# Two halves of shift and scale summed as columns instead of as a row, and eleven stores moved to GpSimd's queue

## The chip, the cores and the metric

The kernel runs on one core of a Trainium2 chip. TensorE (PE) multiplies matrices, VectorE (DVE) and ScalarE (ACT) work on the results, GpSimd (POOL) adds weights, and SyncE (SP) starts most transfers. Each engine runs its own instructions in the order in which the program has them, and waits for the others by semaphores. The metric is the device time of one execution in microseconds (us).

## The reference, cut to what matters

One layer of a diffusion backbone over 1024 latent tokens (and 256 context tokens, which go through the same weights) of 1024 channels. Each sub-layer is normed and modulated by a shift, a scale and a gate, nine rows of 1024 that come from a vector `c`:

```python
mod_lat = (jax.nn.silu(c) @ w_mod[layer] + b_mod[layer])[:, None, :]
ml = jnp.split(mod_lat, N_MOD, axis=-1)
...
x = x + 0.5 * ml[2] * swiglu(modulate(rms_norm(x, norm1_g[layer]), ml[0], ml[1]),
                              ffn1_w_in[layer], ffn1_w_out[layer])
...   # attention and short convolution, second SwiGLU
return rms_norm(x, final_g)
```

`modulate(h, shift, scale)` is `h * (1 + scale) + shift`. So the first product of the whole layer needs the shift `ml[0]` and the scale `ml[1]`, each 1024 values made from a 1024 x 1024 block of `w_mod` (4 MB). All of it is float32.

## The kernel before

Channels lie on partitions: `modl[:, m * 8 + k]` is the column of channels `128 k` to `128 k + 127` of row `m`. A half of a row (512 channels, four columns) is made at a time. At the start the order is:

- `first_mod(1, 0)`: the first half of the scale, latent and context at once. PE multiplies eight chunks of 128 input channels into a row of 512 (`ps`), ACT copies the row (`mrow`), and four PE turns (a transpose of one 128-wide piece each) make columns.
- `second_mod(0, 0, raws00, by_pe=4)`: the first half of the shift, latent only. Half of the input chunks (`k` 0 to 3) are summed by DVE: `macc` is `sum over k of silu(c)[k] * rawm[k]`, still spread over 128 partitions. PE does the chunks 4 to 7 as a row. `macc` is split into two parts (`acch` by ACT, `accl`, the remainder, by DVE), PE adds both over the partitions with a column of ones, and ACT's copy and the four turns follow as above. The result goes into `modl` with the bias `bcol`.
- `second_mod(1, 1, raws11)` and `second_mod(0, 1, raws01)`: the second halves, with all eight chunks on DVE (`by_pe=0`), taken in steps between the first products.

Meanwhile `h`, the modulated first tokens (`xtok`, turned by PE into `ps`, `po`, `pt`), becomes `r` (again two parts, `keep`), and the first feed-forward layer starts. It is computed by a scheme with seven half-size products (class `Winograd`) from pairs of weight column blocks. `start_by_half` computes products 1 and 2 of the first 13 pairs ahead of the rest, on chunks of which only half the channels need to be ready: product 1 is copied to `uc[:, 0]`, product 1 + 2 added into `uc[:, 1]` by DVE. Pairs 0 and 1 stay on the chip; the 11 others are stored by `put_aside` to DRAM (`ucd`) and loaded again later. The latter stores go out on SP's queue, the one that also loads the weights `raw`. POOL's first work, apart from the identity, is the sums `s` of weight blocks for the pairs (`pool.tensor_add`).

Most code is written without an order; a scheduler puts each engine's instructions in order from its own estimates, except those that are pinned (`pinned`, `strict`). So an edit can move neighbours. PSUM banks are a further tie: `ps` has five, `pt` two, `po` one, and a bank is given to the next tile only when the last one was read. Every operation is recorded at line 90, that of the helper which issues it; groups are told apart by the tiles' names.

Of the kernel before, what the change touches and what calls it, by code (L numbers as in the profile page):

```python
# [10 lines left out]
F32R = mybir.dt.float32r  # L11
# [7 lines left out]
P = 128  # L19
D = 1024  # L20
KD = D // P
# [30 lines left out]
def tile_dit_layer(  # L52
# [44 lines left out]
    act, dve, pool, pe, sp = (Engine(e) for e in (nc.scalar, nc.vector, nc.gpsimd, nc.tensor, nc.sync))  # L97
# [11 lines left out]
    def uniq(s):  # L109
        n_tiles[0] += 1  # L110
        return f"{s}_{n_tiles[0]}"
# [4 lines left out]
    def ttile(name, n=512, dt=F32):  # L116
        t = tpool.tile([P, 512], dt, tag="t", name=uniq(name))
        return t[:, :n]
# [4 lines left out]
    def ps_s(n=512):  # L123
        return psum.tile([P, 512], F32, tag="s", name=uniq("ps"), bufs=5)[:, :n]

    def ps_t(n=512):
        return psum.tile([P, 512], F32, tag="t", name=uniq("pt"), bufs=2)[:, :n]
# [4 lines left out]
    def matmul(out, w, x, start, stop, pinned=False, on=False):  # L132

        inst = pe.matmul(out, w, x, start=start, stop=stop, skip_group_check=on)
        if pinned:
            tc.keep_in_program_order(inst)

    def transpose(out, in_, pinned=False):
        n = in_.shape[0]
        inst = pe.transpose(out, in_, ident[:n, :n])  # L140
        if pinned:
            tc.keep_in_program_order(inst)
# [9 lines left out]
    ones = const.tile([P, 1], F32, name="ones")  # L152
    dve.memset(ones[:], 1.0)
    ones_r = const.tile([P, 1], F32R, name="ones_r")
# [4 lines left out]
    bcol = const.tile([P, 72], F32, name="bcol")  # L159
# [26 lines left out]
    def col(name, k=0):  # L186
        o = voff[name] + k
        return cols[:, o : o + 1]

    silu_c = const.tile([P, 16], F32, name="silu_c")  # L190
    act.activation(out=silu_c[:], in_=cols[:, :16], func=AF.Silu)

    modl = const.tile([P, 72], F32, name="modl")
# [3 lines left out]
    def split(src, hi, lo, lo_eng=None, hi_eng=None):  # L197

        if hi_eng is dve:
            dve.tensor_copy(out=hi, in_=src)  # L200
        else:
            act.copy(out=hi, in_=src)
        (lo_eng or dve).tensor_sub(out=lo, in0=src, in1=hi.bitcast(F32))
# [21 lines left out]
    def load_cols(w, o, lo_eng=None, pinned=False):  # L225

        return load_w(w[:, o : o + P].rearrange("(k p) n -> p k n", p=P), (KD, P), lo_eng, pinned)
# [97 lines left out]
    def column_adds(m, half, pm, streams):  # L325
        c0 = m * 8 + half * 4
        for i, v in enumerate(streams):
            dve.tensor_add(
                out=(modl, modc)[v][:, c0 : c0 + 4], in0=pm.rearrange("p (k v) -> p v k", v=len(streams))[:, i],
                in1=bcol[:, c0 : c0 + 4],  # L330
            )
# [18 lines left out]
    def second_mod(m, half, raws, by_pe=0):  # L350


        acc, nk = ttile("macc"), KD - by_pe
        for k in range(nk):
            raw, s = raws[k // 2][:, k % 2], silu_c[:, k : k + 1]
            if k:
                dve.scalar_tensor_tensor(out=acc, in0=raw, scalar=s, in1=acc, op0=ALU.mult, op1=ALU.add)
            else:
                dve.tensor_scalar(out=acc, in0=raw, scalar1=s, scalar2=None, op0=ALU.mult)
            yield  # L360
        ah, al = ttile("acch", dt=F32R), ttile("accl", dt=F32R)
        split(acc, ah, al)
        yield
        pr = ps_s()
        for k in range(nk, KD):
            raw, s = raws[k // 2][:, k % 2], silu_c[:, k : k + 1]
            matmul(pr[:1], s, raw, start=k == nk, stop=False, pinned=True)
            if k in (nk, KD - 1):
                yield
        matmul(pr[:1], ones_r[:], ah, start=not by_pe, stop=False)  # L370
        matmul(pr[:1], ones_r[:], al, start=False, stop=True)
        row = ttile("mrow")
        act.copy(out=row[:1], in_=pr[:1])
        yield
        pm = ps_t(4)
        for j in range(4):
            transpose(pm[:, j : j + 1], row[:1, j * P : (j + 1) * P])
        column_adds(m, half, pm, (0,))
        yield

    def norm_gain(name, m, gname):
# [109 lines left out]
    class Winograd:  # L491
# [228 lines left out]

        def put_aside(self, t):
            ucd = dram.tile([P, 2, 512], F32, name=uniq("ucd"))
            sp.dma_start(out=ucd[:], in_=t[:])
            self.started.append(ucd)

        def start_by_half(self):
# [302 lines left out]
    fetched["b"] = fetch_vectors([("b", b_mod[0])])  # L1029
    raws00 = fetch_mod(0, 0)  # L1030
    mod10, mod00 = first_mod(1, 0, raws10), second_mod(0, 0, raws00, 4)

    def column_pairs(w, offsets):
# [41 lines left out]
    for k in range(4):  # L1075
        if k % 2:
            half1.shifted(h0[k][:, 0], k, xh[k])
        else:
            dve.tensor_scalar(
                out=h0[k][:, 0], in0=xh[k], scalar1=gain1["l"][:, k : k + 1], scalar2=modl[:, k : k + 1],  # L1080
# [3 lines left out]
    start = half1.start_by_half()  # L1084
    run(start, 1)
    for k in range(4):
# [3 lines left out]
        else:  # L1090
            dve.tensor_copy(out=h0[k][:, 1], in_=xt)
    mods1 = (step for m, raws in ((1, raws11), (0, raws01)) for step in second_mod(m, 1, raws))
    turn1 = turn_tokens(C1, t1, ("act", "act"))
    for j in range(2, BY_HALF):
# [144 lines left out]
    for d in range(0, KD, 2):  # L1239
        t = ttile("cx")  # L1240
# [3 lines left out]
        for e in range(2):  # L1244
            for token in range(2):
                at = e * CT + token * P
                transpose(pt[:, at : at + P], c_acc[token][:, (d + e) * P : (d + e + 1) * P])
        for e in range(2):
            te = t[:, e * CT : (e + 1) * CT]
            dve.scalar_tensor_tensor(  # L1250
                out=te, in0=pt[:, e * CT : (e + 1) * CT], scalar=gate1["c"][:, d + e : d + e + 1], in1=te, op0=ALU.mult, op1=ALU.add
# [78 lines left out]
    for i in range(KD):  # L1330
# [6 lines left out]
        for ch, bg, gc in mixed():  # L1337
# [4 lines left out]
            for j in (0, 2):  # L1342
# [3 lines left out]
                    out=ya, in0=u[:, a + j - 1 : b + j - 1], scalar=col(f"w{j}", i), in1=ya, op0=ALU.mult, op1=ALU.add  # L1346
# [372 lines left out]
    for ch in (C0, C1):  # L1719
        o = ch[1]  # L1720
        for d in range(KD):
            w = load_cols(w_out[0], d * P)
# [6 lines left out]
                out=xs(d, ch), in0=ps, scalar=modl[:, 40 + d : 41 + d], in1=xs(d, ch), op0=ALU.mult, op1=ALU.add  # L1729
# [12 lines left out]
        out=gf[:], in0=cols[:, voff["gf"] : voff["gf"] + 8], scalar1=math.sqrt(D), scalar2=None, op0=ALU.mult  # L1742
# [132 lines left out]
```

## Time and profile before

| what | value |
|---|---|
| three runs | 2669.2, 2670.65, 2675.72 us (median 2670.65) |
| the profiled execution | 2670.08 us, its span 2668.3 us |
| TensorE busy | 2633.8 us, 13373 matmul records |
| DVE, ACT, POOL busy | 2002.0, 1173.6, 558.4 us |
| mean granted TensorE clock | 0.996 |

The span runs from the first to the last instruction; times in a timeline count from its start. `x8` stands for that many records of one kind in a row, and an f32 matmul that isn't a transpose leaves two records. The bracket at a row's end gives the idle time of the engine before it and what ended it. A tile's number is left out in the profile and kept in the lists of the order.

### The profile page before, as it was taken

How to read it: one execution, taken by the hardware profiler on the slowest of the kernel's cores; microseconds unless marked ns; L12 is line 12 of the kernel's file. 1: busy time of each engine (PE TensorE's matmuls, PEld its weight loads, DVE VectorE, ACT ScalarE, POOL GpSimd, SP SyncE). 2: the span in 40 equal slices, each digit the busy share in tenths (PEclk: the TensorE clock that was granted, in tenths of full speed). 3: DMA queues.
4: the chain of work that ended last, by engine and by line, in shares of the span. 5: the costliest groups of instructions: out<-in, count | busy, mean ns of one | idle time of the engine just before them, and what ended most of it. 6: DMA issues, size and time to landing. Idle time of an engine off the chain costs nothing.

```text
span 2668.3 us, 36840 instructions
## 1 busy us (share of the span) xinstructions
PE 2633.8 (99%) x13373; PEld 2220.0 (83%) x13373; DVE 2002.0 (75%) x3356; ACT 1173.6 (44%) x2317; POOL 558.4 (21%) x449
## 2 busy tenths in 40 slices
PE   8999999999999999999999999999999999999998
PEld 6787799888778878888999888888888888888888
DVE  5788976788887899877598676685458976657885
ACT  6532454333454643333355576574236333334443
POOL 0134301111020034332033122141001532330200
PEclk9999999999999999999999999999999999999999
DMA  8566475345984355342522432113525643227841
GB/s 320 194 194 189 138 230 158 115 131 187 302 206 119 126 179 173 98 134 72 202 68 92 91 95 62 35 41 98 167 87 171 196 146 97 86 88 285 188 90 64
DMA packets 371471, 381.12 MB, mean 143 GB/s; under 512 B 19526, under 2 KB 258264, under 8 KB 371288
## 3 DMA queue, kind: packets, MB, share of 16 engines
q1 hardware_dynamic: 360472, 357.22, 41.4%
q0 software_dynamic: 10816, 21.53, 4.9%
q8 instruction: 105, 1.72, 0.3%
q14 instruction: 78, 0.64, 0.1%
HBM read 308.88 MB, written 69.76 MB: 142 GB/s over the span
## 4 chain that ended last, share of the span: by engine, by line
PE 90%; DVE 5%; DMA 2%; issue 1%; ACT 1%; POOL 1%; SPq 0%; DVEq 0%; POOLq 0%; ACTq 0%
PE ps L90 74%; PE po L90 8%; PE pt L90 8%; DVE wl L90 1%; DVE r L90 1%; DMA raw<-in_ffn_w_in_dram 1%; DVE nt L90 0%; DMA rawm<-in_w_mod_dram 0%; DMA ws<-in_ffn_w_out_dram 0%; DVE u L90 0%; DVE macc L90 0%; POOL s L90 0%; DVE y L90 0%; POOL sum L90 0%; DVE sq_acc L90 0%
## 5 line engine op out<-in xcount | busy, mean ns | idle before, releaser
L90 PE MATMUL ps<-r,wl 128*128 128x512 f32 x5196 | 1206.8, 391 | 9.6 <-DVE wl L90 3.1
L90 PEld LDWEIGHTS ps<-r,wl 128*128 128x128 f32 x5196 | 974.4, 189 | 218.8 <-DVE wl L90 5.9
L90 ACT CAST wl<-raw 128x512 fp32r<-128x512 f32 x287 | 177.7, 620 | 229.8 <-PE ps L90 173.3
L90 DVE TENSOR_TENSOR wl<-raw,wl 128x512 fp32r<-128x512 f32 x287 | 202.3, 706 | 60.6 <-ACT wl L90 56.7
L90 ACT CAST wl<-sum 128x512 fp32r<-128x512 f32 x168 | 103.2, 620 | 231.9 <-PE ps L90 184.9
L90 DVE TENSOR_TENSOR wl<-sum,wl 128x512 fp32r<-128x512 f32 x168 | 152.2, 908 | 17.8 <-ACT wl L90 16.8
L90 POOL TENSOR_TENSOR sum<-raw 128x512 f32<-128x512 f32 x42 | 60.6, 1443 | 497.9 <-DMA raw<-in_w_in_dram 203.2
L90 DVE SCALAR_TENSOR_TENSOR macc<-rawm,silu_c,macc 128x512 f32<-128x512 f32 x178 | 148.0, 849 | 13.5 <-DMA rawm<-in_w_mod_dram 12.8
L90 DVE TENSOR_TENSOR u<-u,ps 128x512 f32<-128x512 f32 x186 | 126.2, 680 | 33.6 <-PE ps L90 33.6
L90 PE MATMUL ps<-wh,r 128*128 128x256 f32 x768 | 141.6, 284 | 0.0
L90 DVE TENSOR_TENSOR pts<-pt,pts 128x512 fp32r<-128x512 f32 x160 | 108.7, 687 | 41.1 <-ACT pts L90 39.3
L90 ACT CAST pts<-pt 128x512 fp32r<-128x512 f32 x160 | 93.3, 595 | 86.4 <-PE pt L90 82.7
L90 DVE TENSOR_REDUCE m<-ps 128x1 f32<-128x512 f32 (+1 forms) x192 | 110.3, 595 | 23.9 <-PE ps L90 22.3
L90 ACT CAST rh<-hid 128x512 fp32r<-128x512 f32 x132 | 81.3, 620 | 104.6 <-PE ps L90 91.6
L90 PE MATMUL ps<-rh,wl 128*128 128x512 f32 x360 | 122.0, 389 | 0.0
L90 PEld LDWEIGHTS ps<-wh,r 128*128 128x128 f32 x768 | 120.8, 192 | 0.7 <-issue 0.6
L90 POOL TENSOR_TENSOR sum<-raw,sum 128x512 f32<-128x512 f32 x42 | 62.0, 1476 | 268.7 <-DVE wl L90 261.8
L90 ACT CAST wh<-raw 128x512 fp32r<-128x512 f32 (+1 forms) x85 | 67.9, 801 | 103.2 <-PE ps L90 70.2
L90 POOL TENSOR_TENSOR s<-raw 128x512 f32<-128x512 f32 x22 | 32.0, 1457 | 378.5 <-DMA raw<-in_ffn_w_in_dram 297.1
L90 PE MATMUL po<-pts,vh 128*128 128x512 f32 x256 | 110.0, 435 | 0.2 <-ACT pts L90 0.2
L90 PE MATMUL ps<-wl,r 128*128 128x256 f32 x384 | 109.0, 284 | 0.0
L90 DVE TENSOR_TENSOR rl<-hid,rh 128x512 fp32r<-128x512 f32 x132 | 90.3, 686 | 21.7 <-PE ps L90 11.7
(317 smaller groups left out, 5382.9 us busy)
## 6 DMA issues: line engine op xcount, KB each, us to landing
raw<-in_ffn_w_in_dram SPq DMA_DIRECT2D x130, 512.0 KB
raw<-in_ffn_w_out_dram SPq DMA_DIRECT2D x72, 512.0 KB
raw<-in_w_in_dram SPq DMA_DIRECT2D x61, 512.0 KB
rawm<-in_w_mod_dram SPq DMA_DIRECT2D x104, 256.0 KB
hid<-hd SPq DMA_DIRECT2D x40, 512.0 KB
rawm<-in_w_mod_dram SPq DMA_DIRECT2D x32, 512.0 KB
ws<-in_ffn_w_out_dram POOLq DMA_DIRECT2D x30, 512.0 KB, 6.5
ucd<-uc SPq DMA_DIRECT2D x29, 512.0 KB
```

The costliest lines, as they stand in the source:

```text
L90: inst = getattr(self.engine, name)(*args, **kw)
```

## The change

In `second_mod` the copy as a row and the turns go. What was a stationary column of `silu(c)` against 512 moving columns of `rawm` becomes the opposite: a 128 x 128 block of `rawm` is stationary and one column (`silu_c`, or `ones` for `macc`) moves, so that PE writes four columns directly. `macc` is used as it is, in float32, without `acch` and `accl`. The chunks on PE are taken in two pairs, each with four columns of one PSUM tile `pm`, and `macc` has four more. DVE adds `bcol` and the `macc` columns, and then each pair's columns in place. For the second halves there are no pairs. `put_aside` sends its stores to POOL's queue, for this first layer only (`side_from` is set only there).

```diff
@@ second_mod
-        ah, al = ttile("acch", dt=F32R), ttile("accl", dt=F32R)
-        split(acc, ah, al)
         yield
-        pr = ps_s()
-        for k in range(nk, KD):
-            raw, s = raws[k // 2][:, k % 2], silu_c[:, k : k + 1]
-            matmul(pr[:1], s, raw, start=k == nk, stop=False, pinned=True)
-            if k in (nk, KD - 1):
-                yield
-        matmul(pr[:1], ones_r[:], ah, start=not by_pe, stop=False)
-        matmul(pr[:1], ones_r[:], al, start=False, stop=True)
-        row = ttile("mrow")
-        act.copy(out=row[:1], in_=pr[:1])
+        pm = ps_t(4 * (1 + by_pe // 2))
+
+        def columns(at, terms):
+            for j in range(4):
+                for i, (w, x) in enumerate(terms):
+                    matmul(
+                        pm[:, at + j : at + j + 1], w[:, j * P : (j + 1) * P], x, start=i == 0, stop=i == len(terms) - 1,
+                        pinned=True,
+                    )
+
+        for k in range(nk, KD, 2):
+            columns(2 * (k - nk) + 4, [(raws[k // 2][:, i], silu_c[:, k + i : k + i + 1]) for i in range(2)])
+            yield
+        columns(0, [(acc, ones[:])])
         yield
-        pm = ps_t(4)
-        for j in range(4):
-            transpose(pm[:, j : j + 1], row[:1, j * P : (j + 1) * P])
-        column_adds(m, half, pm, (0,))
+        c0 = m * 8 + half * 4
+        out = modl[:, c0 : c0 + 4]
+        dve.tensor_add(out=out, in0=pm[:, :4], in1=bcol[:, c0 : c0 + 4])
+        for i in range(by_pe // 2):
+            dve.tensor_add(out=out, in0=out, in1=pm[:, 4 * i + 4 : 4 * i + 8])
         yield
@@ put_aside
-            sp.dma_start(out=ucd[:], in_=t[:])
+            (pool if self.side_from else sp).dma_start(out=ucd[:], in_=t[:])
```

Beyond about the first 130 us the order of the engines stays as it was, but for a row or two of DVE in the last norm. Three places where it moves:

DVE around the first shift half, before (`macc_245` is its sum, `macc_458` that of the next half, from `rawm_295` and `rawm_297`; `wl_349` and `wh_352` are the parts of the first weights `half`; `h_65_341` is the first modulated tile):

```order
L90 TENSOR_TENSOR gain_l<-gain_l,cols 128x4
L90 TENSOR_TENSOR accl_251<-macc_245,acch_250 128x512
L90 TENSOR_SCALAR macc_458<-rawm_295,silu_c 128x512
L90 SCALAR_TENSOR_TENSOR macc_458<-rawm_295,silu_c,macc_458 128x512
L90 TENSOR_TENSOR modl<-pt_355,bcol 128x4
L90 TENSOR_TENSOR wl_349<-half_292,wl_349 128x512
L90 TENSOR_SCALAR h_65_341<-ps_270,gain_l,modl 128x512
L90 TENSOR_TENSOR wh_352<-half_292,wh_352 128x512
```

And after (the next half's sum is `macc_463`, from `rawm_303` on, the first `h` is `h_63_349`):

```order
L90 TENSOR_TENSOR wl_357<-half_300,wl_357 128x512
L90 TENSOR_TENSOR wh_360<-half_300,wh_360 128x512
L90 TENSOR_SCALAR macc_463<-rawm_303,silu_c 128x512
L90 SCALAR_TENSOR_TENSOR macc_463<-rawm_303,silu_c,macc_463 128x512
L90 TENSOR_TENSOR modl<-pt_250,bcol 128x4
L90 SCALAR_TENSOR_TENSOR macc_463<-rawm_305,silu_c,macc_463 128x512
L90 TENSOR_TENSOR modl<-modl,pt_250 128x4
L90 SCALAR_TENSOR_TENSOR macc_463<-rawm_305,silu_c,macc_463 128x512
L90 TENSOR_TENSOR modl<-modl,pt_250 128x4
L90 SCALAR_TENSOR_TENSOR macc_463<-rawm_307,silu_c,macc_463 128x512
L90 TENSOR_SCALAR h_63_349<-ps_278,gain_l,modl 128x512
```

Both splits of `half` and three more steps of the next sum, on two further `rawm` tiles, now stand ahead of the first `h`.

PE where the second halves of the channels come in, before (`ps_708`, `ps_727` and `ps_796` are product 2 of the first three pairs, `r_139` and `r_140` the third and fourth tile of it; `uc_377` is added to `ps_708` as soon as that is complete):

```order
L90 MATMUL ps_708<-r_140_700,wl_523 128x512
L90 MATMUL ps_727<-r_139_696,wh_630 128x512 x2
L90 MATMUL ps_727<-r_140_700,wh_630 128x512
L90 MATMUL ps_796<-r_139_696,wl_657 128x512
L90 MATMUL ps_708<-r_140_700,wl_523 128x512 x2
```

And after (the same products are `ps_695`, `ps_714` and `ps_783`):

```order
L90 MATMUL ps_695<-r_128_687,wl_519 128x512
L90 MATMUL ps_714<-r_127_683,wh_626 128x512
L90 MATMUL ps_695<-r_128_687,wl_519 128x512 x2
L90 MATMUL ps_714<-r_127_683,wh_626 128x512
L90 MATMUL ps_714<-r_128_687,wh_626 128x512 x3
```

One matmul of another product, not four, now stands between the last three terms of the first product.

POOL's first work after the change (before, the sums `s` stand there alone, and the stores `ucd` stand among the loads of `raw` on SP's queue):

```order
L90 DMA ucd_972<-uc_646 128x1024
L90 TENSOR_TENSOR s_231_1121<-raw_1119 128x512
L90 DMA ucd_1036<-uc_996 128x1024
L90 DMA ucd_1075<-uc_1038 128x1024
L90 TENSOR_TENSOR s_232_1122<-s_231_1121,raw_1117 128x512
L90 TENSOR_TENSOR s_233_1123<-raw_1117,raw_1119 128x512
L90 TENSOR_TENSOR s_232_1122<-raw_1117,s_232_1122 128x512
L90 DMA ucd_1114<-uc_1077 128x1024
L90 DMA ucd_1161<-uc_1116 128x1024
L90 DMA ucd_1198<-uc_1163 128x1024
L90 TENSOR_TENSOR s_266_1294<-raw_1292 128x512
```

Six stores stand ahead of the first sum, two between the first and the second, and three ahead of the next pair's first sum.

## The prediction

> **What bounds the kernel now.** I read the head of the page first, then busy time by stretch, then the timeline of the first 132 us, the only place where the change puts anything; the chain of waits comes last.
>
> ```profile
> span 2668.3 us, 36840 instructions
> PE 2633.8 (99%) x13373; PEld 2220.0 (83%) x13373; DVE 2002.0 (75%) x3356; ACT 1173.6 (44%) x2317; POOL 558.4 (21%) x449
> PE 90%; DVE 5%; DMA 2%; issue 1%; ACT 1%; POOL 1%; SPq 0%; DVEq 0%; POOLq 0%; ACTq 0%
> ```
>
> TensorE is busy 99% of the span and carries 90% of the chain that ended last, so time can only be won where it idles. The busy time by stretch (stretch, its length, then busy us and count of PE, weight loads, DVE, ACT, POOL; granted clock; DMA share; GB/s) shows where:
>
> ```profile
> 20.00:30.00 10.00, 7.75 (x40) 3.63 (x39) 6.08 (x14) 3.68 (x7) 0.00 (x0) 1.00 1.10 376
> 30.00:40.00 10.00, 9.73 (x42) 7.62 (x42) 9.32 (x16) 5.67 (x11) 0.00 (x0) 0.83 1.07 373
> 57.00:66.00 9.00, 6.62 (x44) 4.83 (x42) 5.33 (x18) 8.62 (x18) 0.00 (x0) 0.90 0.52 189
> 74.00:92.00 18.00, 15.69 (x82) 12.84 (x81) 18.00 (x31) 12.03 (x21) 0.00 (x0) 0.99 0.57 200
> 92.00:126.00 34.00, 34.00 (x149) 28.00 (x148) 22.67 (x36) 14.87 (x29) 9.34 (x7) 0.96 0.69 227
> 0.00:130.00 130.00, 119.06 (x560) 90.22 (x561) 88.32 (x165) 75.53 (x133) 10.04 (x13) 0.96 0.75 263
> ```
>
> Over the first 130 us PE idles 130 - 119.06 = 10.9 us. That is all that any change here can win, and 0.3% of the span is 8.0 us. Three holes matter: 20 to 30 us (2.25 idle), 57 to 66 us (2.4 idle, ACT busy 8.62 of 9) and 74 to 92 us (2.3 idle, DVE busy 18.00 of 18). From 92 us on PE is never idle, so what counts is when it resumes there.
>
> **First shift half (20 to 30 us).** The timeline (start, length, engine, operation, tiles; in brackets the idle time before and what ended it):
>
> ```profile
> 21.40 2.73 PE L90 MATMUL ps<-rawm,silu_c 128*1 128x512 f32 x6
> 23.22 0.62 ACT L90 CAST acch<-macc 128x512 fp32r<-128x512 f32 x1 [2.33 <-DVE macc L90]
> 24.84 0.49 DVE L90 TENSOR_SCALAR macc<-rawm,silu_c 128x512 f32<-128x512 f32 x1 [0.28 <-DMA rawm<-in_w_mod_dram]
> 26.53 0.58 ACT L90 COPY mrow<-ps 1x512 f32<-1x512 f32 x1 [2.69 <-PE ps L90]
> 27.16 0.40 PE L90 MATMUL pt<-ident,mrow 1*128 1x1 f32 x4 [0.67 <-ACT mrow L90]
> 28.29 0.80 DVE L90 TENSOR_SCALAR h<-ps,gain_l,modl 128x512 f32<-128x512 f32 x1
> 29.80 0.52 PE L90 MATMUL ps<-r,wl 128*128 128x512 f32 x1 [1.33 <-ACT r L90]
> 2657.71 2.74 PE L90 MATMUL pt<-ones,sq 128*128 128x1 f32 x24
> rawm<-in_w_mod_dram SPq DMA_DIRECT2D x16, 512.0 KB
> ```
>
> *PE work is a wash.* An f32 matmul leaves two records. The 24 records at 2657.71 are the 12 one-column matmuls of the last norm (two column blocks, six squares): 2.74/12 = 0.23 us each. A 512-column row matmul costs 2.73/3 = 0.91 at 21.40. The first shift half trades four of the latter (3.6 us) for 16 one-column ones (3.7 us). In each of the three halves four more one-column matmuls (0.9) stand for two fp32r ones and four turns (0.5 + 0.4). I take zero; both ends are within 0.3 us.
>
> *What leaves the path:* the cast (0.62), its remainder on DVE, the row copy (0.58) and the turns. The column sum needs only `macc` and PE's turn: 16 transposes stand ahead, so it ends near 26.3, against 27.56 for the turns now.
>
> *What is late next:* DVE's own order. It now runs the two `half` splits and the first two `macc` steps of the next half, and puts three further steps of those between the additions into `modl` and ahead of `h`. These steps wait for `rawm` tiles. The first landed at 24.84; a tile is 512 KB, the DMA moves 376 GB/s in this stretch, so the next follow every 1.4 us: 26.2 and 27.6. DVE thus adds `bcol` at 26.4, adds the two column sums after one step each (0.75 with the addition) near 27.1 and 27.9, takes the third step and starts `h` near 28.6 to 28.7. Before it was 28.29: **0.35 us later** at the first product (30.15), although the sum is ready earlier. By the last of the four `h` tiles DVE is 0.4 ahead again, having left out a split of `half` and the remainder; PE reaches 39 us some 0.6 us early (bounds -0.4 to +0.8).
>
> **Second shift half (57 to 66 us).**
>
> ```profile
> 60.00 0.57 ACT L90 COPY mrow<-ps 1x512 f32<-1x512 f32 x1
> 61.06 0.16 DVE L90 TENSOR_TENSOR modl<-pt,bcol 128x4 f32<-128x4 f32 x1 [1.66 <-PE pt L90]
> 61.43 2.93 ACT L90 ACTIVATE h<-h,modl,gain_l 128x512 f32<-128x512 f32 x4
> 61.94 2.74 DVE L90 TENSOR_SCALAR xtok<-xtok,rs_y 128x1024 f32<-128x1024 f32 x4 [0.72 <-PE po L90]
> 65.93 0.78 PE L90 MATMUL ps<-r,wl 128*128 128x512 f32 x1
> ```
>
> Here ACT is the bound: squares and copies of the second tokens stand ahead of the four `h` steps. The change takes one cast and one row copy (0.5 us each in the stream) from ACT, but a weight cast that ACT did before the hole (`wl<-raw`) now stands inside it, between the copies, and the column sum waits for a bank that one of these copies frees, so its result comes near 61.3. I add ACT's rows up to `h` at 61.4 again. The 0.6 us from before end in this hole: zero at 66 us (bounds -1.0, both ACT pieces won, to +0.5).
>
> **The stores (74 to 126 us).**
>
> ```profile
> 72.96 0.84 PE L90 MATMUL ps<-r,wl 128*128 128x512 f32 x3
> 73.84 0.69 DVE L90 TENSOR_TENSOR uc<-uc,ps 128x512 f32<-128x512 f32 x1 [0.86 <-PE ps L90]
> 82.97 0.41 SPq L90 DMA_DIRECT2D ucd<-uc  x1
> 86.66 0.62 ACT L90 CAST wl<-raw 128x512 fp32r<-128x512 f32 x1 [1.60 <-DMA raw<-in_ffn_w_in_dram]
> 89.38 0.62 ACT L90 CAST wl<-raw 128x512 fp32r<-128x512 f32 x1 [1.41 <-DMA raw<-in_ffn_w_in_dram]
> 89.48 0.68 DVE L90 TENSOR_TENSOR nt<-nt,h 128x512 f32<-128x512 f32 x1
> 90.20 0.62 ACT L90 CAST r<-nt 128x512 fp32r<-128x512 f32 x1 [0.20 <-DVE nt L90]
> 91.39 1.07 PE L90 MATMUL ps<-r,wh 128*128 128x512 f32 x2 [2.31 <-ACT wh L90]
> 114.19 0.68 DVE L90 TENSOR_TENSOR uc<-uc,ps 128x512 f32<-128x512 f32 x1
> 118.33 1.30 POOL L90 TENSOR_TENSOR s<-raw 128x512 f32<-128x512 f32 x1 [4.61 <-DMA raw<-in_ffn_w_in_dram]
> 123.31 0.69 DVE L90 TENSOR_TENSOR uc<-uc,ps 128x512 f32<-128x512 f32 x1 [4.14 <-issue]
> 131.22 1.14 ACT L90 CAST wl<-s 128x512 fp32r<-128x512 f32 x2
> L90 POOL DMA_DIRECT2D ws<-in_ffn_w_out_dram x36: 1204/1222/1437, 703.1 to 2560.7; - x36
> ```
>
> PE's wait of 2.31 us before 91.39 ends with a weight cast on ACT that stands behind the cast of `r` at 90.20, and that waits for the DVE step at 89.48. ACT's waits for `raw` (1.60 and 1.41 us) end just before, so they look guilty; but DVE runs 26 operations from 73.84 to 89.48, 0.60 us each without a hole, and sets the end whether `raw` lands sooner or not. So stores off SP's queue win **nothing** on this path, as long as DVE is that full. They cost SP nothing either: `raw` loads there wait for DVE to free a buffer.
>
> What does help is PE's new order before 73.84: the last terms of the first product now stand ahead of three matmuls of other products (0.84/3 = 0.28 at 72.96, about 0.23 in the pace). DVE had waited 0.86 us for that product, so its full stretch starts **0.6 to 0.7 us earlier**, with the same 26 operations, and PE resumes near 90.7. That is the whole gain.
>
> The 11 stores cost POOL 1.22 us each (the last row above: 36 issues elsewhere, with their shortest, median and longest in ns), and POOL has nothing to do before 107. Queued behind them are the sums `s` of the pairs. The last three stores stand ahead of the sum that ran at 118.33, and the third needs the `uc` of 123.31 to 124.0: it ends at 125.2, three sums (1.3 each) at 129.1, and ACT casts them at 131.22. The cover is 2.1 us, so I cost it at nothing; an issue of over 1.22 + 2.1 = 3.3 us would use it up.
>
> [...] No run here shows a store issued from GpSimd beside a full VectorE; the 36 issues above stay within 1.44.
>
> **Sum.** 0 (first half) + 0 (second half) - 0.65 (order before 73.84) + 0 (stores) = -0.65 us against this execution (2670.08 us with what lies around its span of 2668.3): 2669.4. The median of the three runs shown is 2670.65, 0.57 above it, so 2670.0 for the median.
>
> **Rivals.**
> 1. *The stores were the brake.* PE's whole 2.31 us go, and with them both ends of the first halves (1.0): -4 us, 2666.6. For it: ACT's waits for `raw`. Against: the unbroken 0.60 us pace of DVE.
> 2. *Slower: DVE's order lets PE idle longer before 30 us and the clock follows.* PE now waits from 26.3 for the bank that the last addition into `modl` frees (28.0), then again to 30.15: some 3.4 us idle instead of 2.25. The granted clock was 0.83 in the 10 us behind that hole already, which cost 1.7 us; a second stretch like it costs as much again, and together with the 0.35 and a second hole unfilled (0.5) it is +2 to +2.5: 2672.9. It decides if `rawm` lands more than 1 us later than I worked out.
> 3. *Stores starve POOL.* From 3.3 us an issue on, the second pair's sums come late. At 5 us the three stores, of which the first can start at 114.9, end at 129.9 and the sums at 133.8: +2.6, 2672.6; at 6 us 132.9 and 136.8: +5.6, 2675.6. Against: 1.44 was the longest of 36. [...]
> 4. *It changes nothing:* the DVE stretch starts as before, 2670.65.
>
> **Chances.** Forecast 0.45, the stores as brake 0.13, the clock 0.17, starved POOL 0.08, nothing at all 0.12, something unseen 0.05. The range goes from rival 1 with a microsecond of spread between runs (2665.5) to between the two ends of rival 3 (2674.7). The bound for telling a change of this kernel from none is about 0.3%, 8 us; none of these cases reaches it, so same has 0.93, and the rest is the unseen.
>
> **What would show it.** Right: `modl` added three times, `h` at about 28.6, first product near 30.1; second `h` within 0.5 us of 61.4; the first `uc` addition near 73.2; PE resuming near 90.7 with its wait still above 2 us; ACT's waits for `raw` gone without effect. Wrong: a wait of PE below 1 us before 91 (rival 1), a clock below 0.8 between 28 and 42 us (rival 2), store issues on POOL above 3.3 us or ACT waiting for `s` near 131 (rival 3).

## The result: 7 us slower, where 0.65 us faster was forecast

Changed, the kernel takes 2680.27 us (median of 10 runs, 2675.64 to 2682.2) against 2672.54 us before (median of 10 runs, 2669.2 to 2680.99): ratio 1.0026, 95% interval 1.0017 to 1.0035, so 4.5 to 9.4 us more. The change is slower by about 7 us, still under the 0.3% that I took for the bound of what can be told; the interval shows that this bound was too wide. The profiled execution took 2677.11 us (before: 2670.08). The head of its page:

```profile
span 2675.3 us, 36912 instructions
PE 2640.0 (99%) x13403; PEld 2230.9 (83%) x13403; DVE 2003.4 (75%) x3355; ACT 1170.3 (44%) x2311; POOL 568.8 (21%) x460
PE 85%; DVE 4%; DMA 2%; issue 1%; ACT 1%; POOL 1%; SPq 0%; DVEq 0%; ACTq 0%; POOLq 0%
```

TensorE is busy as before, but its 2640.0 us are 6.2 more than the 2633.8 of before. Busy time by stretch, in the columns of the prediction (stretch, length, PE, weight loads, DVE, ACT, POOL, granted clock, DMA share, GB/s):

```profile
20.00:30.00 10.00, 10.00 (x57) 9.19 (x55) 4.73 (x11) 1.81 (x3) 0.00 (x0) 0.66 1.10 376
30.00:40.00 10.00, 6.76 (x28) 5.27 (x28) 9.19 (x18) 4.68 (x8) 0.00 (x0) 0.66 1.07 375
57.00:66.00 9.00, 7.97 (x45) 6.43 (x44) 2.48 (x12) 7.98 (x16) 0.00 (x0) 1.00 0.33 124
74.00:92.00 18.00, 18.00 (x91) 15.04 (x90) 16.76 (x29) 13.31 (x23) 1.81 (x3) 1.00 0.37 124
92.00:126.00 34.00, 30.45 (x124) 24.76 (x124) 26.29 (x42) 16.91 (x31) 8.31 (x10) 0.90 0.67 217
0.00:130.00 130.00, 118.66 (x549) 94.58 (x550) 83.49 (x159) 72.41 (x126) 11.36 (x20) 0.89 0.71 248
```

Over the first 130 us PE is busy as long as before (118.66 against 119.06), and over the span PE's busy time grew by 6.2 us of the 7.0, so the loss is not idle time in the main. The granted clock fell from 0.96 to 0.89. In the first two rows it is 0.66 where it was 1.00 and 0.83, and in the first of these PE is busy without a break: 10.00 of 10.

The timeline of the first half (start, length, engine, operation, tiles; in brackets the idle time before and what ended it) shows the same matmuls at two prices:

```profile
20.78 1.95 PE L90 MATMUL pt<-silu_c,rawm 128*128 128x1 f32 x16
23.01 3.57 PE L90 MATMUL pt<-silu_c,rawm 128*128 128x1 f32 x16
26.44 1.95 PE L90 MATMUL ps<-ident,xtok 128*128 128x128 f32 x8
29.82 0.95 PE L90 MATMUL pt<-ones,macc 128*128 128x1 f32 x8
30.81 0.16 DVE L90 TENSOR_TENSOR modl<-pt,bcol 128x4 f32<-128x4 f32 x1 [4.13 <-PE pt L90]
31.55 0.15 DVE L90 TENSOR_TENSOR modl<-modl,pt 128x4 f32<-128x4 f32 x1
32.34 0.15 DVE L90 TENSOR_TENSOR modl<-modl,pt 128x4 f32<-128x4 f32 x1
33.13 0.80 DVE L90 TENSOR_SCALAR h<-ps,gain_l,modl 128x512 f32<-128x512 f32 x1
34.64 0.79 PE L90 MATMUL ps<-r,wl 128*128 128x512 f32 x1 [1.37 <-ACT r L90]
```

The first sixteen one-column records take 1.95 us, the next sixteen 3.57, and the eight transposes behind them 1.95 where they took 1.09 before. The first product starts at 34.64, not 29.80.

In the traces of before and after the granted clock is 1.00 or 0.50 and nothing between, and the falls and rises within each lie whole stretches of 3.41 us apart (0.50 from 30.14 to 33.56 before, from 22.90 to 29.73 now). Cut along these stretches (the cuts lie 0.2 us early: the clock fell at 22.9, which is why some rows read 0.53 or 0.97), the same view reads as a chain of causes:

```profile
19.30:22.70 3.40, 3.40 (x21) 2.08 (x19) 1.91 (x4) 0.57 (x1) 0.00 (x0) 1.00 1.15 345
22.70:26.10 3.40, 3.40 (x20) 3.38 (x19) 2.91 (x9) 1.24 (x2) 0.00 (x0) 0.53 1.07 399
26.10:29.50 3.40, 3.40 (x18) 3.40 (x18) 0.58 (x1) 0.00 (x0) 0.00 (x0) 0.50 1.08 383
29.50:32.90 3.40, 1.53 (x14) 1.48 (x13) 2.09 (x6) 0.00 (x0) 0.00 (x0) 0.97 1.09 321
32.90:36.30 3.40, 2.03 (x10) 1.48 (x8) 3.40 (x6) 1.92 (x3) 0.00 (x0) 0.54 1.05 407
36.30:39.70 3.40, 3.40 (x11) 2.52 (x11) 3.40 (x7) 2.46 (x5) 0.00 (x0) 0.50 1.10 391
```

Row by row: in the first stretch over half the work is one-column matmuls, and the clock of the next is halved. The second is one-column matmuls but for four narrow turns (0.3 us of them), and the third stays at half. The third holds transposes of 128 columns, and the fourth is back at full. The fourth has the column sum of `macc` and a hole (1.53 busy of 3.4); the fifth falls again. The fifth has a hole too, and the sixth stays at half. The clock records of the two traces give, for the first 130 us, three stretches at half clock before (at 30.1, 64.3 and 91.6 us) and eight now (two each from 22.9, 33.1, 67.3 and 98.0); over the whole span, without the last microseconds, five and nine. Four more, at 1.7 us each where PE sets the pace, come to at most 6.8 of the 7.0 us by which the spans differ. The pair from 98.0 follows a hole of PE (0.36 us busy of the 3 from 95 to 98), not one-column work.

So half clock came behind holes of PE (1.53 us busy of 3.40 ahead of the fall at 33.1, 0.36 of 3.00 ahead of that at 98.0), but also behind a stretch in which TensorE was busy all the time (3.40 of 3.40 in the first row); the runs below say when.

### The profile page after: what moved, and what is told of

Read it like the earlier page. It is cut to its first block, busy times and chain, and to the rows that moved or that the text cites. A ratio compares the mean times of both kernels' runs of the same rounds, so it can differ in the third digit from the quotient of the medians.

```text
span 2675.3 us, 36912 instructions
## 1 busy us (share of the span) xinstructions
PE 2640.0 (99%) x13403; PEld 2230.9 (83%) x13403; DVE 2003.4 (75%) x3355; ACT 1170.3 (44%) x2311; POOL 568.8 (21%) x460
## 4 chain that ended last, share of the span: by engine, by line
PE 85%; DVE 4%; DMA 2%; issue 1%; ACT 1%; POOL 1%; SPq 0%; DVEq 0%; ACTq 0%; POOLq 0%
PE ps L90 70%; PE po L90 8%; PE pt L90 8%; DVE wl L90 1%; DMA rawm<-in_w_mod_dram 0%; DVE macc L90 0%; POOL s L90 0%; DMA ws<-in_ffn_w_out_dram 0%; DVE u L90 0%; DVE r L90 0%; DMA hd<-u 0%; DMA raw<-in_ffn_w_in_dram 0%; DMA raw<-in_ffn_w_out_dram 0%; ACT wl L90 0%; DVE v L90 0%
## 5 line engine op out<-in xcount | busy, mean ns | idle before, releaser
L90 PE MATMUL ps<-kl,qs 128*128 128x512 f32 x384 | 104.2, 395 | 0.0
```

Of the source, the lines that this page charges most:

```text
L90: inst = getattr(self.engine, name)(*args, **kw)
```

## Experiments

Three theories. **T1, the clock:** one-column matmuls keep TensorE busy but count for almost nothing where its clock is set; the lost time is half clock. **R1, the stores:** in the profile of after, ACT waits 3.65 us for a raw weight before 97.19 (1.41 before) and PE waits 3.54 before 98.91 (2.31), so the moved stores may make the loads late. **R2, the order:** DVE's longer list ahead of the first `h`, and the path through PE, delay the first product whatever the clock.

All timings below are against runs of the kernel before on the same chip; a ratio of 1.0010 is 2.7 us. The clock is the mean of the timed executions' granted clocks; the last column counts the 3.41 us stretches at half clock in the first 130 us of the one profiled execution.

| kernel | ratio to before, 95% interval | mean clock | halved stretches |
|---|---|---|---|
| before | 1 | 0.995 | 3 |
| changed | 1.0026 (1.0017 to 1.0035) | 0.9925 | 8 |
| stores alone | 1.0010 (0.9999 to 1.0021) | 0.9953 | 3 |
| stores alone, again | 1.0006 (0.9995 to 1.0017) | 0.9951 | 4 |
| columns alone | 1.0024 (1.0014 to 1.0033) | 0.9923 | 6 |
| columns, first half alone | 1.0026 (1.0015 to 1.0037) | 0.9929 | 7 |
| columns, second halves alone | 1.0014 (1.0005 to 1.0022) | 0.9944 | 5 |
| row for four pieces, columns for the rest | 0.9993 (0.998 to 1.0005) | 0.9948 | 2 |
| columns fed 128 wide | 1.0003 (0.9992 to 1.0014) | 0.9959 | 3 |
| changed, columns fed 128 wide | 0.9995 (0.9987 to 1.0004) | 0.9956 | 1 |

**Stores alone** (the kernel before, one line):

```diff
-            sp.dma_start(out=ucd[:], in_=t[:])
+            (pool if self.side_from else sp).dma_start(out=ucd[:], in_=t[:])
```

> The kernel before with one edit of the change: the first pairs' uc stores are issued by GpSimd instead of SyncE; row copies, turns and halves' sums stay as before. T1 (the clock: each added window of 3.4 us at half clock costs up to 1.7 us, and the one-column matmuls make them): the dips stay those of before (5 windows), PE resumes near 91.4 us, the time is within 1 us of before. R1 (the stores make the raw weights land later: ACT's wait for raw 3.65 us instead of 1.41, PE's wait 3.54 instead of 2.31): PE resumes near 93.3 and the time is +1.5 to +2 us against before. R2 (DVE's order): no change.

2674.39 us against 2674.11. PE resumed at 93.69 us with a wait of 3.47, as R1 had it; but when the same kernel was run again,

> The stores alone, a second time. T1: within 1 us of before. R1: +1.5 to +3 us.

it took 2675.56 against 2674.34, and PE's wait there was 2.32 (17.54 us after DVE's first addition to `uc`; before 17.55). So the long wait comes and goes between executions of one kernel. The two intervals share -0.3 to +4.5 us; what is left of R1 is decided further down.

**Columns alone** (the changed kernel with that line put back):

> The changed kernel with the stores back on SyncE's queue; the column sums stay. T1: the dips stay those of the changed kernel (four windows at half clock in the first 40 us, two near 67, two near 98), time +6 to +7.5 us against before, like the changed kernel within 1 us. R1: +5 us against before, 2 us less than the changed kernel, with ACT's wait for raw near 97 us back at 1.4. R2: as the changed kernel, but with the first product at 34.6 us whatever the clock.

2679.58 against 2674.11: by far most of the loss is in the columns. Six halved stretches rather than the expected eight, first product at 32.43.

**A row for the four pieces that TensorE adds, columns for `macc` and the second halves.** This takes away the 32 one-column records and keeps three of the change's ideas: no split of `macc`, no row for the DVE half, DVE's two-step addition ahead of `h`.

```diff
-        for k in range(nk, KD, 2):
-            columns(2 * (k - nk) + 4, [(raws[k // 2][:, i], silu_c[:, k + i : k + i + 1]) for i in range(2)])
-            yield
-        columns(0, [(acc, ones[:])])
+        if by_pe:
+            pr = ps_s()
+            for k in range(nk, KD):
...
+                matmul(pr[:1], s, raw, start=k == nk, stop=k == KD - 1, pinned=True)
...
+            act.copy(out=row[:1], in_=pr[:1])
+        for j in range(4):
+            matmul(pm[:, j : j + 1], acc[:, j * P : (j + 1) * P], ones[:], start=True, stop=True, pinned=True)
+        if by_pe:
+            for j in range(4):
+                transpose(pm[:, 4 + j : 5 + j], row[:1, j * P : (j + 1) * P], pinned=True)
```

> Stores on SyncE. The four pieces of the first half that TensorE adds are a 1x512 row again by wide matmuls, copied and turned as before; the half's DVE sum macc is summed as columns by ones, and the second halves too. So the sixteen + sixteen one-column matmuls at 20.8 to 26.6 us are gone, while the order of DVE that the columns brought (three additions into modl) largely stays. T1: no half-clock window before 29 us, one instead of two behind it, first product back near 30 us, PE at its second pair of ps near 40 instead of 44.95; time 4 to 6 us below the columns kernel, 0 to +2.5 against before. R2 (the order of DVE and the longer path, not the clock, delays the first product): first product still 33 us or later, time within 1.5 us of the columns kernel.

2673.75 us, 5.8 below the columns alone, with the first product at 31.69. By stretch:

```profile
20.00:30.00 10.00, 8.53 (x47) 4.40 (x45) 6.17 (x15) 2.19 (x4) 0.00 (x0) 1.00 1.10 375
30.00:40.00 10.00, 9.08 (x40) 7.60 (x41) 10.00 (x17) 6.05 (x11) 0.00 (x0) 0.83 1.08 384
0.00:130.00 130.00, 119.71 (x577) 92.16 (x578) 87.05 (x165) 73.54 (x130) 10.38 (x13) 0.97 0.75 264
```

The clock is back at the 1.00 and 0.83 of before, with DVE as full between 30 and 40 us as it could be. R2 is out as the main cause: an order of this kind costs no 5 us.

**Which half?** One kernel has columns in the first half only, one in the two second halves only; the other part is the code of before (`row`; the stores on SyncE). The first, and for the second with the names exchanged:

```diff
+    def second_mod(m, half, raws, by_pe=0):
+        return (second_mod_col if by_pe else second_mod_row)(m, half, raws, by_pe)
```

> Stores on SyncE. Only the first half is summed as columns (the thirty-two one-column records of the four pieces and eight of macc); the two second halves keep the row. T1: +4 to +7 us against before, like the kernel with all columns, with at least two more windows at half clock before 45 us. Rival (the loss lies in the second halves): within 1.5 us of before.

> Stores on SyncE. The first half is summed as before (row, split of macc, copy, turns); only the two second halves are summed as columns by eight one-column records each. T1 (clock, and only the first half has enough one-column work for it): within 1.5 us of before, windows at half clock in the first 130 us as many as before (three, up to four by phase). Rival (the second halves carry part of the loss, as the doubled windows near 67 and 98 us of the changed kernel suggest): +2 to +3.5 us.

The first half alone takes 2680.23 against 2673.73: it has the whole loss. In its profile the clock is at half from 23.4 us for five stretches on end:

```profile
20.00:30.00 10.00, 10.00 (x61) 9.69 (x60) 4.33 (x10) 1.81 (x3) 0.00 (x0) 0.67 1.10 376
30.00:40.00 10.00, 7.22 (x23) 5.49 (x23) 9.72 (x18) 5.23 (x10) 0.00 (x0) 0.50 1.07 376
```

The second halves alone are slower too (2676.53), against T1's expectation, though beside the row in the kernel above the same second halves cost nothing. The parts do not add up to the whole (0.0026 + 0.0014 against 0.0024). The stretches do not begin at the same time in every execution (modulo 3.413 us, the clock changed at 2.84 us before and at 2.42 in the changed kernel), so a hole or a few one-column matmuls could fall into one stretch in this kernel and across two in that; this was not shown.

**What the clock counts.** The kernel before with matmuls into a bank that nobody reads ahead of its first product, one stretch for each width, all f32 with the same 128x128 weights:

```diff
     run(mod00)
+    for w, n in ((512, 22), (1, 130), (512, 22), (128, 90), (512, 22), (256, 60), (512, 22)):
+        filler(raws00[3][:, 0][:, :w], n)
```

> The kernel before with TensorE work into a bank that nobody reads, ahead of the first product, without a gap: 22 matmuls of 512 columns, 130 of one column (30 us at 0.23 us each), 22 of 512, 90 of 128 columns, 22 of 512, 60 of 256, 22 of 512, all f32 with the same 128x128 stationary operand. TensorE is busy all the way. T1: the granted clock falls to 0.5 within 7 us of the start of the one-column stretch and stays there (so it takes near 60 us), and is 1.00 in the 512-column stretches but for one window; 128 and 256 columns tell how wide a matmul has to be. Rival (the clock falls only where TensorE waits): 1.00 throughout, 30 us for the one-column stretch.

Stretches well inside each width: 512 columns, one column, 512, 128, 256.

```profile
30.00:46.00 16.00, 16.00 (x39) 7.07 (x38) 8.61 (x14) 4.53 (x8) 0.00 (x0) 1.00 1.05 393
52.00:94.00 42.00, 42.00 (x199) 42.00 (x198) 0.00 (x0) 0.00 (x0) 0.00 (x0) 0.50 0.00 0
104.00:116.00 12.00, 12.00 (x29) 5.32 (x28) 0.00 (x0) 0.00 (x0) 0.00 (x0) 1.00 0.00 1
120.00:138.00 18.00, 18.00 (x163) 18.00 (x163) 0.00 (x0) 0.00 (x0) 0.00 (x0) 1.00 0.00 1
162.00:178.00 16.00, 16.00 (x76) 14.09 (x75) 0.00 (x0) 0.00 (x0) 0.00 (x0) 1.00 0.00 1
```

PE is busy in every row to the last hundredth, and so is the weight load in the one-column and 128-column rows. Only the one-column row has half clock: 51.2 us of it, fifteen stretches. A record takes 42/199 = 0.211 us there, 18/163 = 0.110 at 128 columns. A second probe, with `(64, 120)`, `(32, 130)` and `(8, 130)` between 512-column ones,

> The probe again with narrower stretches between 512-column ones: 120 matmuls of 64 columns, 130 of 32, 130 of 8. T1: the clock follows the columns fed, so somewhere between 128 (1.00) and 1 (0.50) a width halves it; 8 columns like 1 column (0.50 for nearly the whole stretch), 64 and 32 open. Rival (only the count of matmuls and weight loads matters, which hardly changes with the width): all three 0.50.

reads, in that order, and then just ahead of the two falls of the clock:

```profile
50.00:72.00 22.00, 22.00 (x200) 22.00 (x199) 0.00 (x0) 0.00 (x0) 0.00 (x0) 1.00 0.05 19
100.00:144.00 44.00, 44.00 (x206) 43.85 (x206) 0.00 (x0) 0.00 (x0) 0.00 (x0) 0.50 0.00 0
170.00:214.00 44.00, 44.00 (x208) 44.00 (x208) 0.00 (x0) 0.00 (x0) 0.00 (x0) 0.50 0.00 1
94.00:97.00 3.00, 3.00 (x30) 3.00 (x29) 0.00 (x0) 0.00 (x0) 0.00 (x0) 1.00 0.03 5
166.00:169.00 3.00, 3.00 (x29) 3.00 (x29) 0.00 (x0) 0.00 (x0) 0.00 (x0) 1.00 0.00 0
```

64 columns hold the clock, 32 do not. The last two rows are of 32 and 8 columns ahead of the falls at 97.85 and 169.53: still at full clock, they hold some 30 records in 3 us, no fewer than the 27 at 64 columns (200 in 22 us). PE, weight loads and the count of both were alike, so the rival is out: in these probes the clock goes by how many columns are fed. Where between 32 and 64 the limit lies, and how a stretch of mixed widths is counted, was not measured.

**The same sums, fed 128 wide.** If that is so, each column can be repeated, so that the clock holds while everything else stays. Group j writes columns j to j+127 of the bank, and the next group overwrites all but column j:

```diff
-                        pm[:, at + j : at + j + 1], w[:, j * P : (j + 1) * P], x, start=i == 0, stop=i == len(terms) - 1,
-                        pinned=True,
+                        pm[:, at + j : at + j + P], w[:, j * P : (j + 1) * P], x.to_broadcast([P, P]),
+                        start=i == 0, stop=i == len(terms) - 1, pinned=True,
```

The columns of `macc`, which are fed last, move behind those of the pairs in the bank, so that they do not overwrite them. Once with the stores on SyncE, once in the changed kernel as it is:

> The columns kernel (stores on SyncE), the same matmuls in the same places, but each fed with its column repeated 128 times: group j writes columns j to j+127 of the bank, the next group overwrites all but column j. A record of 128 columns takes 0.137 us (the transposes at full clock) against 0.122 for one column: 56 records in all three halves, +0.8 us of work. T1 (the clock falls because a one-column matmul counts as next to no activity; the probe showed 1.00 at 128 columns): no window at half clock before 29 us, two or three single ones before 130 us, time 5 to 8 us below the columns kernel, i.e. -2 to +1 us against before. Rival (the path through the column sums, or DVE's order, is what costs the 5 us): within 1.5 us of the columns kernel, +4.5 to +7 against before.

> The changed kernel, stores on GpSimd as it has them, with each column of the sums fed 128 times instead of once. T1 (one-column matmuls and the clock carry the whole loss): like the kernel with 128-column sums and the stores on SyncE, 0 to +2 us against before, 5 to 8 below the changed kernel. R1 (the stores carry 1.5 to 3 us beside it): +2 to +5 against before.

2674.51 against 2673.05, and 2673.16 against 2674.34. The scheduler's order moved as well: on PE four turns now stand ahead of the first product, and on DVE the first `h` comes after three steps of the next `macc`, not five. So `h` starts 1.66 and 1.67 us behind the first addition to `modl`; in the columns kernel and the changed one it was 2.32. The changed kernel, fed 128 wide:

```profile
21.16 2.05 PE L90 MATMUL pt<-silu_c,rawm 128*128 128x128 f32 x16
23.48 2.05 PE L90 MATMUL pt<-silu_c,rawm 128*128 128x128 f32 x16
...
20.00:30.00 10.00, 8.73 (x67) 7.18 (x65) 6.18 (x17) 1.81 (x3) 0.00 (x0) 1.00 1.10 375
30.00:40.00 10.00, 8.12 (x40) 6.24 (x40) 10.00 (x17) 6.88 (x12) 0.00 (x0) 1.00 1.08 381
0.00:130.00 130.00, 117.77 (x591) 92.85 (x592) 85.81 (x164) 72.84 (x127) 15.72 (x24) 0.99 0.75 263
```

The first two rows are of the timeline, the others of busy time by stretch. Sixteen records of 128 columns take 2.05 us, 0.10 more than sixteen of one column at full clock and 1.52 less than at half. With that the ratio goes from 1.0026 to 0.9995, and this kernel still holds the moved stores, the three additions into `modl` and three of the five steps ahead of `h`. The one-column feed carries the loss: what the order gave back ahead of `h` is 0.65 us, against 5.6 us between the two column kernels and 8 between the two changed ones. (The intervals of the first pair just touch, 1.0014 and 1.0014; those of the second lie apart.) R1 and what is left of R2 have no more than the interval leaves (-3.5 to +1.1 us for both together). In this profile, with the stores moved, PE resumed at 91.22, 17.57 us after DVE's first addition to `uc` (73.65), as before (17.55).

**Can the holes be filled?** Four kernels got 512-column matmuls into an unread bank, to hold the clock where PE waits. First, in the columns kernel, one behind each pair and three behind the sum of `macc`:

```diff
+    def filler(x, n):
+        junk = ps_s()
+        for _ in range(n):
+            matmul(junk, ident[:], x, start=True, stop=True, pinned=True)
...
             columns(2 * (k - nk) + 4, [(raws[k // 2][:, i], silu_c[:, k + i : k + i + 1]) for i in range(2)])
+            filler(raws[k // 2][:, 0], 1)
...
     run(mod00)
+    filler(raws00[3][:, 0], 3)
```

> The columns kernel (stores on SyncE) with 512-column matmuls of ident into a bank that nobody reads: one behind each pair's sixteen column matmuls and three behind the macc columns of the first half. That is about 5 x 0.9 = 4.5 us more of TensorE work, 3.6 of it in stretches where TensorE is full. T1 (the clock falls because one-column matmuls and the hole count as too little activity): the four half-clock windows of the first 40 us fall to one or none, and the time is 1 to 5 us below the columns kernel in spite of the added work. Rival (the delay is the work and the order itself): +1.7 to +4.5 us above the columns kernel.

2680.57 against 2674.11, no gain, although the profile shows one halved stretch in the first 40 us instead of three and the mean clock rose to 0.9941. The five fillers took 5.98 us by the timeline (rows of 1.10, 2.06 and 2.82), 2.06 of it at half clock: it seems that what the clock gave, the added work took. Next, two fillers in the first hole of the kernel with the row (only the last line of that diff, with 2 for 3),

> The kernel with the row for the four pieces and columns for macc and the second halves (which ran at the time of before), with two 512-column matmuls into a bank that nobody reads behind the turns of the first half, where TensorE otherwise waits 1.07 and 1.32 us before its first product. T1 (a hole of that size is what halves the clock near 30 us): the window near 30 us is gone and the time is 1 to 2 us below that kernel. Rival (the phase of the window or the work behind decides): no gain, 0 to +1 us.

2671.59 against 2673.73, ratio 0.9995 (0.9987 to 1.0004), mean clock 0.9964; the same line in the kernel fed 128 wide,

> As the kernel with 128-column sums, and two 512-column matmuls into a bank that nobody reads in the hole behind the first half's sum. T1: the window near 30 us is gone as well; 1 to 2 us below the kernel with 128-column sums, 1 to 3.5 below before. Rival: the fillers stand in the way, 0 to +1.5.

2672.82 against 2673.05, ratio 1.0001 (0.9993 to 1.0010), 0.9964; and, from the first of these two, sums of `macc` fed 128 wide and `filler(acc, 1)` behind the last of them, in the second hole:

> The kernel with the row for the four pieces and two fillers in the first hole, and now each column of the macc sums fed 128 times, and one 512-column matmul into a bank that nobody reads behind the last half's sum, in the hole near 61 us. T1: the window near 64 us goes as well as that near 30; 2 to 4 us below before. Rival: the filler delays the turns behind it, or the window falls elsewhere: within 1 us of the kernel with the first hole filled alone (which ran at 0.9995 of before).

2675.93 against 2674.34, ratio 1.0006 (0.9998 to 1.0014), 0.9962. In the profile of the first of the last three the aimed-at stretch was at full clock: two records of a product took 0.72 us at 32.06, where before they took 1.20 at 31.78. In none of the four did the time follow. No kernel beat the one before by more than its interval.

## Why the prediction was wrong

*"PE work is a wash."* This is the step that failed. The price was right at full clock: in the columns kernel the 32 records took 1.95 + 1.99 = 3.94 us, against 3.7 by the 0.23 us of the last norm and 3.6 for the rows they replace. What I left out is that a busy TensorE can lose its clock, as it did at 22.9 us (0.50 behind a stretch with PE busy 3.40 of 3.40). I read the granted clock as an effect of idle time alone, and so I asked of the change only what it did to the holes. For the same reason my 10.9 us of idle time were not, as I wrote, all that could move in the first 130 us: a clock of 0.96 over 130 us is another 5.2. The term of zero measured +5.6 us in one pair (columns alone 1.0024, fed 128 wide 1.0003) and +8 in the other (changed 1.0026, fed 128 wide 0.9995); in each, up to some 0.65 can be the order of DVE instead.

*Rival 2, the clock.* Its sign came true (0.66 between 30 and 40 us, below the 0.8 that I had named), at a chance of 0.17, but its mechanism was not the one that acted. It had the clock fall behind a longer hole of PE before 30 us, one stretch more, +2 to +2.5 us. It fell at 22.9, with PE busy 10.00 of 10 between 20 and 30; the hole came after, and with five more halved stretches in the first 130 us the price was threefold.

*First half otherwise.* The additions into `modl` came as forecast: three of them, one step of `macc` apart (0.74 and 0.79), then `h` 0.79 later. But they began at 30.81, not 26.4, mostly since the pieces and transposes ahead ran at half clock; the first product was 4.84 late, not 0.35 (0.6 of it a later start: the turn of `vraw` ahead of the pieces stood at 18.76, before at 18.18). Fed 128 wide, at full clock, the additions began at 28.20, still 1.8 later than forecast: 1.0 of that is again the start (19.14), and the other 0.8 is about the column matmuls of `macc` (1.06 us there), for which my 26.3 had left hardly any time behind the 16 transposes (these ended at 26.0 before). The product started at 31.74, 1.6 later than forecast, with four turns now ahead of it.

*Second half.* `h` started at 67.61, 6.18 late, of which 5.4 was there before (PE's run of ten matmuls began at 44.95, not 39.56). I had forecast zero.

*Order before 73.84.* Right: DVE's wait for the first product went from 0.86 to 0.33, half a microsecond. In the changed kernel it cannot be seen in the time: in its profile DVE's first addition to `uc` stands at 79.50, 5.7 us late.

*Stores.* Right that they win nothing, and no sum of POOL's was held up by a long issue: issues on POOL took 0.53 to 0.73 us, less than the 1.22 that I took.

```profile
84.41 0.73 POOL L90 DMA_DIRECT2D ucd<-uc  x1 [83.10 <-DVE r L90]
95.57 0.53 POOL L90 DMA_DIRECT2D ucd<-uc  x1 [4.88 <-DVE uc L90]
97.19 0.62 ACT L90 CAST wl<-raw 128x512 fp32r<-128x512 f32 x1 [3.65 <-DMA raw<-in_ffn_w_in_dram]
98.91 1.22 PE L90 MATMUL ps<-r,wh 128*128 128x512 f32 x2 [3.54 <-ACT wh L90]
```

Rival 3 put an issue at 5 or 6 us, and no run shows such an issue (1.44 was the longest before): three of the eleven fell between 74 and 92 us, where VectorE was busy 16.76 of 18 us, and took 0.53 to 0.73. What I had said would be gone, ACT's waits for `raw`, grew here: PE resumed 19.41 us after DVE's first addition to `uc` (79.50), not 17.55, so that 1.9 us of this one execution lie there, at a granted clock of 1.00, and are not the clock's. DVE, whose full stretch was my reason why late loads could not matter, was busy 16.57 of the 18.50 us from 79.50 to 98.00. The repeat of the stores alone shows that these waits vary from one execution to the next. Whether the stores cost a microsecond or none is not settled.

*The sum.* With the clock held, the change comes to -1.3 us (-3.5 to +1.1) by the ratio of the kernel fed 128 wide, an interval that contains the forecast of -0.65; that the change wins anything is not shown. Without it, the sum missed one term some ten times as large as all the others. The range was built from rivals of +2 to +5.6 us, and none of them let the halves of the clock multiply.

## What to carry over

Count the columns fed, not only TensorE's busy time: here 1.95 us of one-column f32 matmuls in a stretch of 3.41 us were followed by a clock of 0.50 (in the probes it was 0.50 in runs of 1, 8 and 32 columns), and that tail cost more (7 us) than the matmuls (3.9). Where a narrow matmul has to stand in a row of its own kind, repeat its column to 64 or 128: in the probe 64 columns took 22/200 = 0.110 us a record, no more than one column here (1.95/16 = 0.122), and in this kernel 128 turned a loss of 7 us into none. Read the granted clock in steps of 3.41 us beside what TensorE did in the step before; a busy share of 99% hides it.

## What the hardware did that I had not expected

- In the two probes the granted clock follows the columns fed: 1.00 at 64, 128, 256 and 512 columns, 0.50 at 1, 8 and 32, f32, with TensorE busy throughout (42.00 us of 42 at one column, 22.00 of 22 at 64), and at 128 columns and fewer its weight loads too (43.85 of 44 at the least).
- Transposes of 128 columns count: the stretch from 26.10 to 29.50 holds nothing else but the last one-column records, at half clock, and the next row reads 0.97 (full clock from 29.7 on).
- The clock also goes with most of the spread between executions. Over the 30 runs of before that stand beside the first experiments, the span goes from 2667.6 us (clock 0.997) to 2683.9 (0.992); a least-squares line gives 0.96 us of span for each microsecond of span times (1 - clock), with a correlation of 0.81, so some two thirds of the variance.
- Holding the clock with unread work is no free gain: fillers raised the mean clock from 0.9923 to 0.9941, from 0.9948 to 0.9964 and from 0.9959 to 0.9964, and the time did not follow.
